# A chunked state-space scan rebuilt: blocks of eight chunks with 16 neighbouring columns, a doubling over the block ends, then the ends carried into the next block

## The chip, the cores and the metric

One core of one Trainium2 chip. The engines are TensorE (PE; its weight loads are listed as PEld), VectorE (DVE), ScalarE (ACT), GpSimd (POOL) and SyncE (SP), which issues most of the transfers. The metric is the device time of one execution in microseconds, the median of several runs.

## The reference, cut to what matters

One layer of a decoder: adaLN, a combined input projection, an S5 state-space branch beside a sliding-window attention branch, an output projection, then a gated MLP with a short convolution. x is (1, 1024, 1024) in float32. The change concerns the S5 branch alone. It has 32 groups of 16 channels, and each group drives 64 complex states through a linear recurrence over the 1024 positions:

```python
bu_re = jnp.einsum("blgh,gph->blgp", ug, bb_re)
bu_im = jnp.einsum("blgh,gph->blgp", ug, bb_im)
def combine(e1, e2):
    a1r, a1i, b1r, b1i = e1
    a2r, a2i, b2r, b2i = e2
    return (a2r * a1r - a2i * a1i,
            a2r * a1i + a2i * a1r,
            a2r * b1r - a2i * b1i + b2r,
            a2r * b1i + a2i * b1r + b2i)
_, _, s_re, s_im = lax.associative_scan(combine, (a_re_t, a_im_t, bu_re, bu_im), axis=1)
y = (jnp.einsum("blgp,ghp->blgh", s_re, c_re.astype(f32))
     - jnp.einsum("blgp,ghp->blgh", s_im, c_im.astype(f32))
     + d_skip.astype(f32).reshape(N_SSM_GROUPS, SSM_GROUP) * ug)
z = jax.nn.gelu(y.reshape(bsz, seq, D_SSM))
out = z * jax.nn.sigmoid(z @ w_glu.astype(f32) + b_glu.astype(f32))
```

## The kernel before

The 1024 positions are cut into 128 chunks of T = 8. Inside a chunk the recurrence is a small matrix (the local kernel); between chunks only the state at a chunk's end is carried. So the S5 branch has these stages. (1) The input U of each group is transposed, chunks along the free side, into UT (lines 534 to 548); ScalarE adds the shift Bu while it evacuates. (2) Products of WJ and UT give each chunk's contribution to the state, the injections, real in SR and imaginary in SI, for 16 pairs of groups and 128 chunks, with a column of zeros ahead (lines 562 to 579). (3) The scan over the 128 chunks, on VectorE (lines 645 to 681): a doubling up and down (six levels each), in which a step multiplies the columns at a power of two apart by a power of the transition and adds them to others. The helper cmac does it in pairs of instructions: a product into PSUM bank 7 (`bk<-tS,ep` in the rows), and its sum into the scan's tile (`tS<-tS,bk`). The powers stand in ep. (4) An exchange between the two halves of the partitions (lines 706 to 711). (5) For each group, y is the local kernel WI times UT plus the output matrix CA times the state, in PSUM, and its GELU on ScalarE gives zc (lines 714 to 726), which is transposed back into zT (lines 727 to 736). After it come the GLU (tanh on ScalarE, line 771), the split into high and low parts for the products, and the output projection.

Beside this run the attention heads: six projection tiles, three products each (high and low parts), then a norm per head on VectorE and ScalarE (head_w, head_out), and 16 attention units of four heads each (lines 811 to 861), whose exponentials are issued after the last GELU.

The local kernel needs a way over DRAM: ka, in tile A12, is written to kd by four transfers (line 623) and read back as WI (line 700). The relative-position bias takes the same way over vd (lines 603 to 605 and 629).

Tiles are named by tags; two uses of one tag share a buffer, and the later waits until the earlier is done. A scheduler decides the order of the instructions on each engine from the data they need. TensorE's order is pinned as written from line 524 to 581.

Of the kernel before, what the change touches and what calls it, by code (L numbers as in the profile page):

```python
# [20 lines left out]
NC_ = L // T  # L21
# [24 lines left out]
def pick(name, i):  # L46
    return PICK[name][i % len(PICK[name])]
# [15 lines left out]
def hymba_kernel(ctx, tc, xT, c, wmod, wu, wkvq, small, consts, relb, pq, wglu, wout, wup, wdn, out):  # L63
    nc = tc.nc
    pool = ctx.enter_context(tc.tile_pool(name="sb", bufs=1))
    pp = ctx.enter_context(tc.tile_pool(name="ps", bufs=1, space=bass.MemoryType.PSUM))
    dp = ctx.enter_context(tc.tile_pool(name="dr", bufs=1, space=bass.MemoryType.DRAM))
    bank = [pp.tile([128, 512], F32, name=f"bk{i}") for i in range(8)]
    SIZES = {"HA": 2048, "HB": 2048, "S16": 4128, "XQ": 4096}

    def new(tag, dt=F32):
        return pool.tile([128, SIZES.get(tag, 1024)], dt, tag=tag, name="t" + tag)

# [13 lines left out]
    vec, act, pol, sync = nc.vector, nc.scalar, nc.gpsimd, nc.sync  # L87
# [29 lines left out]
    def tt(eng, o, a, b, op):  # L117
        return eng.tensor_tensor(out=o, in0=a, in1=b, op=op)  # L118
# [106 lines left out]
    Bu = pool.tile([128, 32], F32, name="Bu")  # L225
# [13 lines left out]
    for k in range(8):  # L239
# [6 lines left out]
        w = half(newr(f"U{k}") if k < 4 else wux[:, (k - 4) * 1024:(k - 3) * 1024])  # L246
# [71 lines left out]
    PWr = pool.tile([128, 288], F32, name="PWr").rearrange("p (g d) -> p g d", d=9)  # L318
    PWi = pool.tile([128, 288], F32, name="PWi").rearrange("p (g d) -> p g d", d=9)
# [113 lines left out]
    for i in range(4):  # L433
        tmp = new("A10") if i == 3 else IB[i + 1]
# [102 lines left out]
    UTt = [None] * 4  # L537

    def emit_ut(i):
        if i % 2 == 0:  # L540
            UTt[i // 2] = new(f"A{5 + i // 2}")
        b = abank()
        for q in range(4):
            g = 4 * i + q
            pe.transpose(b[:, q * 128:(q + 1) * 128], U[:, g * 128:(g + 1) * 128], ident)
        for q in range(4):
            g = 4 * i + q
            act.activation(out=UTt[i // 2][:, (g % 8) * 128:(g % 8 + 1) * 128], in_=b[:, q * 128:(q + 1) * 128], func=AF.Identity, bias=Bu[:, g:g + 1])

    for i0, n_ in ((0, 4), (4, 2), (6, 2)):  # L550
        for i in range(i0, i0 + n_):
# [8 lines left out]
        return WJt[g // 8][:, (g % 8) * 128:(g % 8 + 1) * 128]  # L560

    scan = new("S16")
    SR = scan[:, 0:2064].rearrange("p (g c) -> p g c", c=129)
    SI = scan[:, 2064:4128].rearrange("p (g c) -> p g c", c=129)
    for i in range(4):
        br_, bi_ = abank(), abank()
        for q in range(4):
            for par in range(2):
                g = 2 * (4 * i + q) + par
                ps = slice(par * 64, par * 64 + 64)  # L570
                pe.matmul(br_[ps, q * 128:(q + 1) * 128], WJ(g)[:, 0:64], UT(g), start=True, stop=True)
                pe.matmul(bi_[ps, q * 128:(q + 1) * 128], WJ(g)[:, 64:128], UT(g), start=True, stop=True)
        next(h0)
        evac(SR[:, 4 * i:4 * i + 4, 1:129], br_.rearrange("p (g c) -> p g c", c=128), "I")
        if i != 1:
            next(h0)
        evac(SI[:, 4 * i:4 * i + 4, 1:129], bi_.rearrange("p (g c) -> p g c", c=128), "I")
    vec.memset(SR[:, :, 0:1], 0.0)
    vec.memset(SI[:, :, 0:1], 0.0)

    pst.close()

# [39 lines left out]
    for q in range(4):  # L622
        sync.dma_start(out=kd[:, 8 * q:8 * q + 8, 112:240],
                       in_=ka[32 * q:32 * q + 16, :].rearrange("p (g x) -> p g x", x=128))
# [17 lines left out]
        head_out(t, h, b)  # L642


    ep = pool.tile([128, 14 * 16], F32, name="ep")
    er = [ep[:, 16 * i:16 * i + 16] for i in range(6)]
    ei = [ep[:, 96 + 16 * i:112 + 16 * i] for i in range(6)]
    et = ep[:, 192:208]
    for par in range(2):
        ps = slice(par * 64, par * 64 + 64)  # L650
        vec.tensor_copy(out=er[0][ps, :], in_=PWr[ps, par:32:2, 8])
        vec.tensor_copy(out=ei[0][ps, :], in_=PWi[ps, par:32:2, 8])
    for l in range(1, 6):
        tt(vec, er[l], er[l - 1], er[l - 1], MUL)
        tt(vec, et, ei[l - 1], ei[l - 1], MUL)
        tt(vec, er[l], er[l], et, SUB)
        tt(vec, et, er[l - 1], ei[l - 1], MUL)
        tt(vec, ei[l], et, et, ADD)

    def cmac(l, dst, src, n):  # L660
        step = max(1, 512 // n)
        for g0 in range(0, 16, step):
            g1 = min(16, g0 + step)
            shp = [128, g1 - g0, n]
            tp = bank[7][:, 0:(g1 - g0) * n].rearrange("p (g c) -> p g c", c=n)
            e_r = er[l][:, g0:g1].rearrange("p (g o) -> p g o", o=1).to_broadcast(shp)
            e_i = ei[l][:, g0:g1].rearrange("p (g o) -> p g o", o=1).to_broadcast(shp)
            sr, si = SR[:, g0:g1, src], SI[:, g0:g1, src]
            dr, di = SR[:, g0:g1, dst], SI[:, g0:g1, dst]
            for d_, e_, s_, op in ((dr, e_r, sr, ADD), (dr, e_i, si, SUB), (di, e_r, si, ADD), (di, e_i, sr, ADD)):  # L670
                tt(vec, tp, s_, e_, MUL)
                tt(vec, d_, d_, tp, op)

    for l in range(6):
        s = 1 << l
        n = NC_ // (2 * s)
        cmac(l, slice(2 * s, 2 * s * n + 1, 2 * s), slice(s, 2 * s * (n - 1) + s + 1, 2 * s), n)
    for l in range(5, -1, -1):
        s = 1 << l
        n = NC_ // (2 * s) - 1  # L680
        cmac(l, slice(3 * s, 3 * s + 2 * s * (n - 1) + 1, 2 * s), slice(2 * s, 2 * s * n + 1, 2 * s), n)


    QS = {}
    for h in range(2):
        for i in range(4):
            q_ = newr(f"H{8 + 4 * h + i}")
            for kv in range(2):
                p0, p1 = slice(kv * 64, kv * 64 + 64), slice(64 - kv * 64, 128 - kv * 64)
                q = q_[:, kv * 512:kv * 512 + 512]  # L690
                QS[i, kv, h] = q
                src = qn[i][p0, h * 512:h * 512 + 512]
# [12 lines left out]

    for i in range(2):
        sw = new(f"U{4 + i}")[0:64, :].rearrange("p (g c) -> p g c", c=128)
        a_, b_ = SR[:, 8 * i:8 * i + 8, 1:129], SI[:, 8 * i:8 * i + 8, 1:129]
        act.copy(sw, a_[64:128])
        vec.tensor_copy(out=a_[64:128], in_=b_[0:64])  # L710
        act.copy(b_[0:64], sw)
# [4 lines left out]
    for i in range(8):  # L716
        b = bank[int(pick("YB", i))]
        for q in range(4):
            g = 4 * i + q
            o = b[:, q * 128:(q + 1) * 128]  # L720
            st = (SI if g % 2 else SR)[:, g // 2, 0:128]
            pe.matmul(o, UT(g), WI(g), start=True, stop=False)
            pe.matmul(o, st, CA(g)[:, 16:144], start=False, stop=True)
        zo = zc[i // 2].rearrange("p (t g h) -> p g t h", t=8, h=16)[:, 4 * (i % 2):4 * (i % 2) + 4]
        yb = b.rearrange("p (g t h) -> p g t h", t=8, h=16)
        gelus.append(act.activation(out=zo, in_=yb, func=AF.Gelu_apprx_tanh).ins)
    zTt = new("S16")
    zT = [zTt[:, m * 1024:(m + 1) * 1024] for m in range(4)]
    for m in range(4):
        zv = zT[m].rearrange("p (c t) -> p t c", t=8)  # L730
        for q2 in range(2):
            b = sbank()
            for q in range(4):
                t_ = 4 * q2 + q
                pe.transpose(b[:, q * 128:(q + 1) * 128], zc[m][:, t_ * 128:t_ * 128 + 128], ident)
            evac(zv[:, 4 * q2:4 * q2 + 4, :], b.rearrange("p (t c) -> p t c", t=4), "Z")

    cact2 = new("X4")
    sync.dma_start(out=cact2, in_=cad.partition_broadcast(128))
# [24 lines left out]
    for h in range(2):  # L764
        hs = slice(h * 512, h * 512 + 512)
        for n in range(4):
            b = sbank()
# [6 lines left out]
        for n in range(4):  # L774
            src = zT[n][:, hs]
# [31 lines left out]
    hp = ctx.enter_context(ExitStack())  # L807
    hp.enter_context(tc.high_priority(0))
    yT = [[new(f"U{2 * h + j}").rearrange("p (i t) -> p i t", i=2) for j in range(2)] for h in range(2)]
    att = pool.tile([128, 16 * 20], F32, name="att")  # L810
    for n in range(8):
        av = bank[2]
        for kv in range(2):
# [30 lines left out]
            for kb in range(nb):  # L844
                b = bank[3 + kb]
# [528 lines left out]
```

## Time and profile before

| | us |
|---|---|
| median of three runs | 1128.36 (1127.03 to 1128.59) |
| the profiled execution, its own time | 1126.86 |
| its span from the first to the last instruction | 1125.1 |
| TensorE busy in it | 1045.2 |
| VectorE busy | 923.1 |
| ScalarE busy | 581.7 |
| GpSimd busy | 275.7 |

The shares of the whole span mix stages with different limits. The stage of the scan lies between 95 and 275 us, and the rows below are from there. A timeline row gives the start in us, the time of the instruction or of a run of alike instructions (x and their number), the engine, the line, the operation with what it writes and reads, and in brackets how long the engine stood idle before it and what ended that.

### The profile page before, as it was taken

Reading aid. Unit: us, or ns where it says so; the run is one execution under the profiler, and the core shown is the slowest. Engines: PE = TensorE matmul, PEld = TensorE weight load, DVE = VectorE, ACT = ScalarE, POOL = GpSimd, SP = SyncE. Lnnn points to the kernel's source line nnn. Section 1 sums busy time; section 2 is a strip of 40 time slices with the busy share of each in tenths; the row PEclk is TensorE's granted clock in tenths of the full one; section 3 lists DMA queues with packets and bytes.
Section 4 is the critical chain, followed back from the end, with each engine's and each line's share of the span. In section 5 each row is a group of like instructions: output and inputs, shape, how many; then the busy total and the mean of one; then the engine's idle time right before and its main releaser. Section 6 shows DMA issues by size and latency. Waiting matters only on the chain.

```text
span 1125.1 us, 13333 instructions
## 1 busy us (share of the span) xinstructions
PE 1045.2 (93%) x4692; PEld 825.7 (73%) x4692; DVE 923.1 (82%) x1489; ACT 581.7 (52%) x1008; POOL 275.7 (25%) x165
## 2 busy tenths in 40 slices
PE   6979999589989799879999999999999999989998
PEld 4877777376656577657888888888888778768876
DVE  7994899958889587888777888887787888997985
ACT  5415443478896366636554545455545474434342
POOL 0000000001233102763222323221312033564541
PEclk9989999788999899979999999999999999999999
DMA  9501516014028855322223232332221449622012
GB/s 365 223 24 38 110 59 92 2 40 167 1 65 229 245 184 148 103 94 94 94 76 113 94 131 94 131 112 94 76 94 57 168 166 419 126 45 31 1 38 113
DMA packets 49638, 128.14 MB, mean 114 GB/s; under 512 B 6273, under 2 KB 14241, under 8 KB 49570
## 3 DMA queue, kind: packets, MB, share of 16 engines
q1 hardware_dynamic: 44962, 118.89, 31.0%
q0 software_dynamic: 4608, 8.39, 4.8%
q8 instruction: 37, 0.61, 0.2%
q14 instruction: 31, 0.25, 0.1%
HBM read 105.28 MB, written 21.99 MB: 113 GB/s over the span
## 4 chain that ended last, share of the span: by engine, by line
PE 46%; DVE 10%; issue 1%; DMA 1%; ACT 1%; POOL 0%; DVEq 0%; ACTq 0%; POOLq 0%
PE bk L97 45%; DVE tH L118 3%; DVE tA L118 2%; DVE tU L118 2%; DVE tX L127 1%; PE bk L99 1%; DMA tX<-in_dram 1%; DVE tX L118 1%; DVE tS L118 1%; DVE tXQ L127 0%; DVE tW L127 0%; DMA tW<-in_dram 0%; DVE tHA L118 0%; DVE tHB L118 0%; POOL tH L118 0%
## 5 line engine op out<-in xcount | busy, mean ns | idle before, releaser
L97 PE MATMUL bk<-tA,tU 128*128 128x512 f32 x516 | 127.2, 395 | 0.0
L97 PE MATMUL bk<-tU,tU 128*128 128x512 f32 x516 | 121.9, 390 | 1.6 <-DVE tU L118 1.1
L97 PE MATMUL bk<-tH,tU 128*128 128x512 f32 x477 | 116.0, 392 | 0.0
L97 PEld LDWEIGHTS bk<-tU,tU 128*128 128x128 f32 x516 | 96.5, 188 | 23.4 <-DVE tU L118 2.6
L97 PEld LDWEIGHTS bk<-tA,tU 128*128 128x128 f32 x516 | 97.0, 188 | 22.7
L97 PEld LDWEIGHTS bk<-tH,tU 128*128 128x128 f32 x477 | 89.1, 188 | 19.3
L127 DVE SCALAR_TENSOR_TENSOR tX<-tH,sm,tX 128x1023 f32<-128x1023 f32 x66 | 99.3, 1504 | 3.5 <-ACT tX L1100 3.4
L97 PE MATMUL bk<-tA,tXQ 128*128 128x512 f32 x300 | 74.5, 395 | 0.7 <-ACT tH L1053 0.7
L99 PE MATMUL bk<-tH,tU 128*128 128x512 f32 x267 | 65.7, 402 | 2.4 <-DVE tU L118 2.4
L133 ACT CAST tU<-tW 128x512 fp32r<-128x512 f32 (+1 forms) x67 | 47.1, 710 | 38.7 <-PE bk L97 18.2
L97 PEld LDWEIGHTS bk<-tA,tXQ 128*128 128x128 f32 x300 | 56.3, 188 | 14.2 <-ACT tH L1053 1.2
L118 POOL TENSOR_TENSOR tU<-tW,tU 128x512 fp32r<-128x512 f32 x25 | 36.1, 1455 | 114.9 <-ACT tU L133 93.2
L99 PEld LDWEIGHTS bk<-tH,tU 128*128 128x128 f32 x267 | 50.9, 193 | 15.4 <-DVE tU L118 3.2
L118 POOL TENSOR_TENSOR tXQ<-tW,tXQ 128x512 fp32r<-128x512 f32 x12 | 49.0, 4086 | 52.2 <-ACT tXQ L133 37.0
L118 DVE TENSOR_TENSOR tX<-tX,tX 128x512 f32<-128x512 f32 (+1 forms) x61 | 59.4, 976 | 1.0 <-DMA tX<-in_dram 0.2
L97 PE MATMUL bk<-tH,tA 128*128 128x512 f32 (+1 forms) x156 | 55.5, 487 | 5.0 <-ACT tH L133 2.1
L118 POOL TENSOR_TENSOR tH<-tH,att 128x1024 f32<-128x1024 f32 (+1 forms) x9 | 17.0, 1889 | 173.2 <-DVE att L841 153.3
L118 DVE TENSOR_TENSOR tU<-tW,tU 128x512 fp32r<-128x512 f32 (+2 forms) x43 | 37.7, 878 | 17.7 <-ACT tU L133 17.7
L97 PE MATMUL bk<-tXQ,tH 128*128 128x256 f32 (+2 forms) x224 | 50.2, 367 | 1.7 <-DVE att L829 1.6
L118 POOL TENSOR_TENSOR tU<-tX,tU 128x512 fp32r<-128x512 f32 x19 | 31.0, 1632 | 80.7 <-ACT tU L133 66.6
L97 PEld LDWEIGHTS bk<-tXQ,tH 128*128 128x128 f32 x224 | 44.4, 267 | 8.3 <-DVE att L829 4.4
L118 DVE TENSOR_TENSOR tU<-tX,tU 128x512 fp32r<-128x512 f32 x37 | 28.9, 788 | 23.6 <-ACT tU L133 23.6
(355 smaller groups left out, 2440.5 us busy)
## 6 DMA issues: line engine op xcount, KB each, us to landing
tW<-in_dram SPq DMA_DIRECT2D x49, 512.0 KB, 3.4
tX<-in_dram SPq DMA_DIRECT2D x47, 512.0 KB, 3.3
tS<-in_dram SPq DMA_DIRECT2D x30, 512.0 KB, 7.4
gd<-tX SPq DMA_DIRECT2D x22, 512.0 KB, 2.8
tA<-in_dram SPq DMA_DIRECT2D x12, 512.0 KB, 9.8
tH<-in_dram SPq DMA_DIRECT2D x12, 512.0 KB, 4.9
tH<-gd SPq DMA_DIRECT2D x8, 512.0 KB, 9.1
tA<-gd SPq DMA_DIRECT2D x8, 512.0 KB, 10.1
```

Of the source, the lines that this page charges most:

```text
L97: return f(*a, **k)
L99: i = f(*a, **k)
L118: return eng.tensor_tensor(out=o, in0=a, in1=b, op=op)
L127: return vec.scalar_tensor_tensor(out=o, in0=a, scalar=s, in1=b, op0=op0, op1=op1)
L133: act.copy(o, i)
```

## The change

The tile of the scan has another layout: real or imaginary (t), 16 pairs of groups (g), the chunk's place r in its block of eight, and the block q, 16 of them, with q innermost. So the 16 blocks are neighbouring columns. UT is written in that order, by r and then q; each injection's evacuation is cut into two copies (places 1 to 7 of all blocks, and place 0 of the next block), since the states are kept one chunk later; one memset on GpSimd clears the first column.

The scan has three parts. Six steps go from place r - 1 to place r for all 16 blocks, and a seventh carries the last place into the next block's place 0. Four steps double over the 16 block ends. Seven steps carry the ends into the other places. Each step is seven instructions: four products into mt, a tile in SBUF with the tag A12, one sum over both real and imaginary parts, and two over one part. The powers 1 to 8 of the transition over a chunk, and then 16, 32 and 64 of them, are made by epow. The exchange, the y products and the evacuation of zT read the new layout. The small tiles att and brow share a buffer.

```diff
-    SIZES = {"HA": 2048, "HB": 2048, "S16": 4128, "XQ": 4096}
+    SIZES = {"HA": 2048, "HB": 2048, "S16": 4096, "XQ": 4096}
...
-            act.activation(out=UTt[i // 2][:, (g % 8) * 128:(g % 8 + 1) * 128], in_=b[:, q * 128:(q + 1) * 128], func=AF.Identity, bias=Bu[:, g:g + 1])
+            act.activation(
+                out=UTt[i // 2][:, (g % 8) * 128:(g % 8 + 1) * 128].rearrange("p (r q) -> p q r", r=8), in_=b[:, q * 128:(q + 1) * 128].rearrange("p (q r) -> p q r", r=8),
+                func=AF.Identity, bias=Bu[:, g:g + 1],
+            )
...
+    SC = scan.rearrange("p (t g r q) -> p t g r q", t=2, g=16, r=8)
+    def evac_inj(t, i, b):
+        v = b.rearrange("p (g e q) -> p g e q", e=8, q=16)
+        evac(SC[:, t, 4 * i:4 * i + 4, 1:8, :], v[:, :, 0:7, :], "I")
+        evac(SC[:, t, 4 * i:4 * i + 4, 0, 1:16], v[:, :, 7, 0:15], "I")
...
-    vec.memset(SR[:, :, 0:1], 0.0)
-    vec.memset(SI[:, :, 0:1], 0.0)
+    pol.memset(SC[:, :, :, 0, 0:1], 0.0)
...
-    def cmac(l, dst, src, n):
-        step = max(1, 512 // n)
-        for g0 in range(0, 16, step):
-            g1 = min(16, g0 + step)
-            shp = [128, g1 - g0, n]
-            tp = bank[7][:, 0:(g1 - g0) * n].rearrange("p (g c) -> p g c", c=n)
...
-            for d_, e_, s_, op in ((dr, e_r, sr, ADD), (dr, e_i, si, SUB), (di, e_r, si, ADD), (di, e_i, sr, ADD)):
-                tt(vec, tp, s_, e_, MUL)
-                tt(vec, d_, d_, tp, op)
-    for l in range(6):
-        s = 1 << l
-        n = NC_ // (2 * s)
-        cmac(l, slice(2 * s, 2 * s * n + 1, 2 * s), slice(s, 2 * s * (n - 1) + s + 1, 2 * s), n)
-    for l in range(5, -1, -1):
...
+    def cmac(k, dst, src, n, tmp):
+        w = 16 * n
+        shp = [128, 16, n]
+        e_r, e_i = [v[:, k, :].rearrange("p (g o) -> p g o", o=1).to_broadcast(shp) for v in (epr, epi)]
+        ab_ = [[tmp[:, (2 * j + t) * w:(2 * j + t + 1) * w].rearrange("p (g q) -> p g q", q=n) for t in range(2)] for j in range(2)]
+        for t in range(2):
+            tt(vec, ab_[0][t], src[:, t], e_r, MUL)
+        tt(vec, ab_[1][0], src[:, 1], e_i, MUL)
+        tt(vec, ab_[1][1], src[:, 0], e_i, MUL)
+        both = tmp[:, 0:2 * w].rearrange("p (t g q) -> p t g q", t=2, q=n)
+        tt(vec, dst, dst, both, ADD)
+        tt(vec, dst[:, 0], dst[:, 0], ab_[1][0], SUB)
+        tt(vec, dst[:, 1], dst[:, 1], ab_[1][1], ADD)
+    mt = new("A12")
+    for r in range(2, 8):
+        cmac(0, SC[:, :, :, r, :], SC[:, :, :, r - 1, :], 16, mt)
+    cmac(0, SC[:, :, :, 0, 1:16], SC[:, :, :, 7, 0:15], 15, mt)
+    for l in range(4):
         s = 1 << l
+        cmac(7 + l, SC[:, :, :, 0, 1 + s:16], SC[:, :, :, 0, 1:16 - s], 15 - s, mt)
+    for r in range(1, 8):
+        cmac(r - 1, SC[:, :, :, r, 1:16], SC[:, :, :, 0, 1:16], 15, mt)
...
-        a_, b_ = SR[:, 8 * i:8 * i + 8, 1:129], SI[:, 8 * i:8 * i + 8, 1:129]
+        a_, b_ = [SC[:, t, 8 * i:8 * i + 8].rearrange("p g r q -> p g (r q)") for t in range(2)]
...
-            st = (SI if g % 2 else SR)[:, g // 2, 0:128]
+            st = SC[:, g % 2, g // 2].rearrange("p r q -> p (r q)")
...
-        zv = zT[m].rearrange("p (c t) -> p t c", t=8)
+        zv = zT[m].rearrange("p (q r t) -> p t r q", r=8, t=8)
```

The order of the instructions moves at three places that matter here. The first is VectorE's queue where the scan begins; tX are the heads' tiles, tA_892 and tA_899 are ka, tA_1493 is mt, tS_774 the scan's tile, bk_70 is bank 7. Before:

```order
L118 TENSOR_TENSOR tX_607<-bk_65,tX_362 128x512 [waits PE_49]
L118 TENSOR_TENSOR bk_70<-tS_774,ep 128x512 [waits DVE_49]
L118 TENSOR_TENSOR tS_774<-tS_774,bk_70 128x8x64 [waits DVE_49]
L118 TENSOR_TENSOR bk_70<-tS_774,ep 128x512 [waits DVE_49]
L118 TENSOR_TENSOR tS_774<-tS_774,bk_70 128x8x64 [waits DVE_49]
L118 TENSOR_TENSOR bk_70<-tS_774,ep 128x512 [waits DVE_49]
L118 TENSOR_TENSOR tA_892<-tA_892,ddt 128x8x16 [waits Activation_49]
L118 TENSOR_TENSOR tS_774<-tS_774,bk_70 128x16x32 [waits DVE_49]
```

Now:

```order
L118 TENSOR_TENSOR tX_607<-bk_65,tX_362 128x512 [waits PE_49]
L118 TENSOR_TENSOR tA_899<-tA_899,ddt 128x8x16 [waits Activation_49]
L127 SCALAR_TENSOR_TENSOR tX_601<-bk_68,tX_601 128x512 [waits PE_49,Activation_49]
L127 SCALAR_TENSOR_TENSOR tX_602<-tX_601,tX_602 128x512 [waits DVE_49]
L127 SCALAR_TENSOR_TENSOR tX_607<-tX_607,bcol,tX_602 128x512 [waits DVE_49]
L118 TENSOR_TENSOR tA_1493<-tS_774,ep 128x256 [waits DMAHW6_49,DMAHW7_49,DMAHW5_49,DMAHW4_49]
L118 TENSOR_TENSOR tA_1493<-tS_774,ep 128x256 x3
L122 TENSOR_SCALAR tX_607<-tX_607,kq 128x512 [waits DVE_49]
L118 TENSOR_TENSOR tX_607<-bk_66,tX_362 128x512 [waits PE_49]
L118 TENSOR_TENSOR tS_774<-tS_774,tA_1493 128x32x16 [waits DVE_49]
L118 TENSOR_TENSOR tU_1096<-tW_1093,tU_1095 128x1024 [waits Activation_49]
```

The first product of the scan stands behind the sum into ka, the first norm of the heads and four DMA queues, where before the scan's first level ran among them.

The second is TensorE's queue where the injections' operands are transposed; `cn` is the identity, tA_562 the second tile of IB, tS_382 is U, tHA and tHB are the first operands of the head product in bank 64. Before:

```order
L99 MATMUL bk_68<-cn,tA_561 128x128 x4
L97 MATMUL bk_64<-tHA,tU_1001 128x512 [waits Activation_49]
L97 MATMUL bk_64<-tHA,tU_1001 128x512
L99 MATMUL bk_69<-cn,tA_562 128x128 [waits DVE_49]
L99 MATMUL bk_69<-cn,tA_562 128x128 x3
L99 MATMUL bk_67<-cn,tA_562 128x128 x4
L99 MATMUL bk_68<-cn,tS_382 128x128 [waits Activation_49]
L99 MATMUL bk_68<-cn,tS_382 128x128 x3
```

Now (the rows end where the transposes begin again):

```order
L97 MATMUL bk_64<-tH_91,tU_1008 128x512
L97 MATMUL bk_64<-tH_92,tU_1008 128x512
L97 MATMUL bk_64<-tH_91,tU_1009 128x512
L97 MATMUL bk_64<-tH_93,tU_1008 128x512
L97 MATMUL bk_64<-tH_94,tU_1008 128x512
L97 MATMUL bk_64<-tH_93,tU_1009 128x512
L97 MATMUL bk_64<-tH_95,tU_1008 128x512
L99 MATMUL bk_69<-cn,tA_562 128x128 [waits DVE_49]
L99 MATMUL bk_69<-cn,tA_562 128x128 x3
L99 MATMUL bk_67<-cn,tA_562 128x128 x4
L99 MATMUL bk_68<-cn,tS_382 128x128 [waits Activation_49]
```

These twelve transposes stood after two of the head's products and stand after 19 of them now.

The third is ScalarE's queue at the end of the scan; L709 and L711 (before), L731 and L733 (now) are the exchange, L726 and L748 the GELU, L836 and L857 the attention's exponential. Before:

```order
L711 COPY tS_774<-tU_1649 64x8x128 [waits DVE_49,Activation_49]
L726 ACTIVATE tX_1655<-bk_69 128x4x8x16 [waits PE_49]
L726 ACTIVATE tX_1655<-bk_68 128x4x8x16 [waits PE_49]
L726 ACTIVATE tX_1656<-bk_69 128x4x8x16 [waits PE_49,Activation_49]
L836 ACT_TABLE_LOAD
L836 ACTIVATE att<-att 128x4 [waits DVE_49]
```

Now:

```order
L731 COPY tU_1678<-tS_774 64x1024 [waits DVE_49,Pool_49]
L731 COPY tU_1682<-tS_774 64x1024
L733 COPY tS_774<-tU_1678 64x1024 [waits DVE_49]
L733 COPY tS_774<-tU_1682 64x1024 [waits DVE_49]
L748 ACT_TABLE_LOAD
L748 ACTIVATE tX_1686<-bk_69 128x4x8x16 [waits PE_49]
L748 ACTIVATE tX_1686<-bk_70 128x4x8x16 [waits PE_49]
```

Both halves' exchanges stand together ahead of all eight GELUs, where the second half's stood behind four of them.

## Rows read from the trace of the kernel before

**Rows 1.** Table of stretches: limits, length, busy us (instructions) per engine, clock, DMA.

```profile
116.30:140.00 23.70, 23.70 (x221) 18.88 (x220) 22.36 (x32) 9.72 (x17) 0.00 (x0) 1.00 0.58 114
140.00:203.60 63.60, 57.81 (x292) 44.30 (x290) 61.45 (x128) 23.88 (x37) 0.00 (x0) 0.99 0.40 71
203.60:230.20 26.60, 19.11 (x69) 13.64 (x70) 25.45 (x48) 17.00 (x26) 0.00 (x0) 0.63 0.00 1
...
248.00:273.00 25.00, 22.71 (x98) 16.59 (x99) 18.16 (x52) 24.69 (x62) 1.89 (x1) 0.75 0.44 148
350.00:400.00 50.00, 43.23 (x169) 30.51 (x168) 35.10 (x58) 21.49 (x34) 11.41 (x12) 0.93 0.85 241
```

**Rows 2.** Timeline of VectorE, scan and heads, 116 to 230 us.

```profile
116.36 0.70 DVE L118 TENSOR_TENSOR bk<-tS,ep 128x512 f32<-128x512 f32 x1 [6.80 <-ACT tS L133]
...
137.64 0.68 DVE L118 TENSOR_TENSOR tX<-bk,tX 128x512 f32<-128x512 f32 x1
...
138.63 1.22 DVE L118 TENSOR_TENSOR tU<-tW,tU 128x1024 fp32r<-128x1024 f32 x1
...
139.97 1.05 DVE L118 TENSOR_TENSOR bk<-tS,ep 128x512 f32<-128x512 f32 x1
...
229.51 0.68 DVE L118 TENSOR_TENSOR tS<-tS,bk 128x504 f32<-128x504 f32 x1
```

**Rows 3.** VectorE: scan groups by width (busy us, mean ns), then two timeline rows.

```profile
L118 DVE TENSOR_TENSOR bk<-tS,ep 128x512 f32<-128x512 f32 x12 | 10.0, 832 | 7.7 <-ACT tS L133 7.3
L118 DVE TENSOR_TENSOR tS<-tS,bk 128x512 f32<-128x512 f32 x12 | 9.9, 821 | 0.3
...
L118 DVE TENSOR_TENSOR tS<-tS,bk 128x16 f32<-128x16 f32 x4 | 0.7, 186 | 0.1
...
92.94 0.45 DVE L118 TENSOR_TENSOR tA<-tU,PWr 128x288 f32<-128x288 f32 x1
55.12 9.10 DVE L118 TENSOR_TENSOR tA<-tU,PWi 128x1024 f32<-128x1024 f32 x8
```

**Rows 4.** SyncE's timeline from the bias table to kd; a transfer's us to landing.

```profile
128.60 0.36 SPq L605 DMA_DIRECT2D vd<-tA  x1
...
134.51 0.36 SPq L629 DMA_DIRECT2D tA<-vd  x1
135.00 1.85 SPq L623 DMA_DIRECT2D kd<-tA  x4
...
kd<-tA SPq DMA_DIRECT2D x4, 64.0 KB, 3.7
```

**Rows 5.** Timeline of ScalarE: activations into UT, a plain and a strided copy.

```profile
101.95 3.20 ACT L548 ACTIVATE tA<-bk,Bu 128x128 f32<-128x128 f32 x12 [3.31 <-PE bk L99]
...
154.37 0.57 ACT L133 COPY tA<-bk 128x512 f32<-128x512 f32 x1
...
247.90 1.10 ACT L133 COPY tS<-bk 128x512 f32<-128x512 f32 x1
```

**Rows 6.** Timeline of ScalarE, TensorE and GpSimd from the exchange on.

```profile
204.34 1.04 ACT L709 COPY tU<-tS 64x1024 f32<-64x1024 f32 x1 [0.59 <-DVE tH L118]
...
225.28 0.63 PE L97 MATMUL bk<-tHA,tA 128*128 128x128 f32 x2
...
231.28 0.39 PE L97 MATMUL bk<-tA,tS 128*128 128x128 f32 x2
...
240.92 1.28 ACT L836 ACT_TABLE_LOAD   x1
...
245.49 0.60 ACT L133 CAST tHB<-tW 128x512 fp32r<-128x512 f32 x1
...
247.41 0.60 ACT L726 ACTIVATE tX<-bk 128x512 f32<-128x512 f32 x1
...
244.54 1.04 POOL L118 TENSOR_TENSOR tH<-tH,att 128x512 f32<-128x512 f32 x1 [131.87 <-DVE att L841]
...
355.56 2.77 POOL L118 TENSOR_TENSOR tH<-tH,att 128x1024 f32<-128x1024 f32 x1
```

More of the change, by code (lines that the diff above doesn't have):

```diff
@@ L456, in hymba_kernel @@
     bcol = pool.tile([128, 6], F32, name="bcol")
-    brow = pool.tile([2, 128 * 2], F32, name="brow")
+    att = pool.tile([128, 16 * 20], F32, name="att")
+    brow = att[0:2, 64:320]
     def head_w(t):
@@ L562, in hymba_kernel @@
     scan = new("S16")
-    SR = scan[:, 0:2064].rearrange("p (g c) -> p g c", c=129)
-    SI = scan[:, 2064:4128].rearrange("p (g c) -> p g c", c=129)
+    SC = scan.rearrange("p (t g r q) -> p t g r q", t=2, g=16, r=8)
[3 more added lines that the diff above has]
+        evac(SC[:, t, 4 * i:4 * i + 4, 0, 1:16], v[:, :, 7, 0:15], "I")
     for i in range(4):
@@ L573, in hymba_kernel @@
         next(h0)
-        evac(SR[:, 4 * i:4 * i + 4, 1:129], br_.rearrange("p (g c) -> p g c", c=128), "I")
+        evac_inj(0, i, br_)
         if i != 1:
             next(h0)
-        evac(SI[:, 4 * i:4 * i + 4, 1:129], bi_.rearrange("p (g c) -> p g c", c=128), "I")
-    vec.memset(SR[:, :, 0:1], 0.0)
-    vec.memset(SI[:, :, 0:1], 0.0)
+        evac_inj(1, i, bi_)
+    pol.memset(SC[:, :, :, 0, 0:1], 0.0)
     pst.close()
@@ L642, in hymba_kernel @@
         head_out(t, h, b)
[L645 to L648, printed above, removed]
+    ep = pool.tile([128, 416], F32, name="ep")
+    epr = ep[:, 0:176].rearrange("p (n g) -> p n g", g=16)
+    epi = ep[:, 176:352].rearrange("p (n g) -> p n g", g=16)
     for par in range(2):
         ps = slice(par * 64, par * 64 + 64)
-        vec.tensor_copy(out=er[0][ps, :], in_=PWr[ps, par:32:2, 8])
-        vec.tensor_copy(out=ei[0][ps, :], in_=PWi[ps, par:32:2, 8])
@@ L653, in hymba_kernel @@
[L653 to L658, printed above, removed]
-    def cmac(l, dst, src, n):
-        step = max(1, 512 // n)
-        for g0 in range(0, 16, step):
-            g1 = min(16, g0 + step)
-            shp = [128, g1 - g0, n]
-            tp = bank[7][:, 0:(g1 - g0) * n].rearrange("p (g c) -> p g c", c=n)
[L666 to L669, printed above, removed]
-            for d_, e_, s_, op in ((dr, e_r, sr, ADD), (dr, e_i, si, SUB), (di, e_r, si, ADD), (di, e_i, sr, ADD)):
-                tt(vec, tp, s_, e_, MUL)
-                tt(vec, d_, d_, tp, op)
@@ L674, in hymba_kernel @@
-    for l in range(6):
-        s = 1 << l
-        n = NC_ // (2 * s)
-        cmac(l, slice(2 * s, 2 * s * n + 1, 2 * s), slice(s, 2 * s * (n - 1) + s + 1, 2 * s), n)
-    for l in range(5, -1, -1):
-        s = 1 << l
-        n = NC_ // (2 * s) - 1
-        cmac(l, slice(3 * s, 3 * s + 2 * s * (n - 1) + 1, 2 * s), slice(2 * s, 2 * s * n + 1, 2 * s), n)
+        vec.tensor_copy(out=epr[ps, 0, :], in_=PWr[ps, par:32:2, 8])
+        vec.tensor_copy(out=epi[ps, 0, :], in_=PWi[ps, par:32:2, 8])
@@ new lines, in epow @@
+    def epow(dst, n, src, by):
+        o = ep[:, 352:352 + 16 * n].rearrange("p (n g) -> p n g", g=16)
+        xr, xi = epr[:, src:src + n], epi[:, src:src + n]
+        yr, yi = [v[:, by:by + 1].to_broadcast([128, n, 16]) for v in (epr, epi)]
+        dr, di = epr[:, dst:dst + n], epi[:, dst:dst + n]
+        tt(vec, dr, xr, yr, MUL)
+        tt(vec, o, xi, yi, MUL)
+        tt(vec, dr, dr, o, SUB)
+        tt(vec, di, xr, yi, MUL)
+        tt(vec, o, xi, yr, MUL)
+        tt(vec, di, di, o, ADD)
@@ new lines, in hymba_kernel @@
+    for args in ((1, 1, 0, 0), (2, 2, 0, 1), (4, 4, 0, 3), (8, 1, 7, 7), (9, 1, 8, 8), (10, 1, 9, 9)):
+        epow(*args)
+    def cmac(k, dst, src, n, tmp):
[11 more added lines that the diff above has]
+        tt(vec, dst[:, 1], dst[:, 1], ab_[1][1], ADD)
@@ L735, in hymba_kernel @@
                 pe.transpose(b[:, q * 128:(q + 1) * 128], zc[m][:, t_ * 128:t_ * 128 + 128], ident)
-            evac(zv[:, 4 * q2:4 * q2 + 4, :], b.rearrange("p (t c) -> p t c", t=4), "Z")
+            evac(zv[:, 4 * q2:4 * q2 + 4], b.rearrange("p (t r q) -> p t r q", t=4, r=8), "Z")
     cact2 = new("X4")
@@ L809, in hymba_kernel @@
     yT = [[new(f"U{2 * h + j}").rearrange("p (i t) -> p i t", i=2) for j in range(2)] for h in range(2)]
-    att = pool.tile([128, 16 * 20], F32, name="att")
     for n in range(8):
```

## The prediction

> **What bounds the kernel now.** I read the table of stretches first [rows 1]. [...] From 248 to 273 us ScalarE is the bound: 24.69 of 25.00. The chain of waits, followed back from the end, stops long before it reaches this place, so the scan has to be followed by hand, from the rows of each engine in order of time. The scan's first instruction starts at 116.36 and its last at 229.51, ending at 230.2 [rows 2].
>
> **The change part by part.**
>
> *The scan's own work.* Before: 112 VectorE instructions in 22 groups of one width, of which the first and the last are shown [rows 3]; their busy times add up to 62.6 us. A pair with columns at distance 2 costs 0.70 us for 512 elements (one at 116.36) [rows 2], at distance 4 it costs 1.05 (one at 139.97) [rows 2]. After: 18 steps of 7 instructions, 126 in all: in six steps four products of 256 elements, one sum over 512 and two over 256; in eight steps 240 and 480; in four steps 224, 208, 176, 112 and their doubles. All of them run over neighbouring columns. Prices: 0.45 us for 288 elements [rows 3], 0.70 for 512, which is about 1.1 ns an element and 0.13 fixed; so 0.42 for 256, 0.41 for 240, 0.66 for 480. A full step is 6 x 0.42 + 0.70 = 3.2 us, one of 240 is 3.1, the four narrow ones together 10.4. Sum: 6 x 3.2 + 8 x 3.1 + 10.4 = 54.6 us. That is the upper bound. The lower: eight instructions of 1024 elements that wait for nothing take 9.10 us, 1.14 each, where one alone is listed with 1.22 [rows 3], so about 0.08 of an instruction lies under the next; for up to 110 of the 126 that makes 46. So the scan saves 8 to 16.5 us of VectorE; I take 14, since about half of the new instructions carry no wait and the heads' work stands between the others. [...]
>
> *The powers of the transition* (36 small instructions in place of 25) lie in VectorE's idle time ahead of 116 us, where only the scan's input is awaited (idle 6.80) [rows 2]. Cost 0; without that cover 11 more at 0.19, the price of 16 elements [rows 3], some 2 us.
>
> *A new wait.* The products went into PSUM bank 7, which nobody else used then. Now they go into tile A12, which holds the local kernel matrix (ka) until four writes have carried it to kd. The order shows the first product waiting for four DMA queues. Those writes are issued at 135.00 to 136.85, behind the first bias load at 134.51, which itself waits for the bias table's write issued at 128.60; the last of them lands 3.7 us after its issue at about 136.4 [rows 4]. So the scan can't start before T0 = 140.1, where before it started at 116.36. Behind the waiting product in VectorE's queue stand three head instructions that before ran from 137.64 to 139.85, 2.2 us [rows 2], among them the low half of the next head's weights, for which TensorE waits. What VectorE did by 140 and now does after it: 24 scan instructions of 512 elements (10.0 + 9.9 us [rows 3]) less the two that came after (2.1), that is 17.8, and the 2.2 of heads.
>
> *What feeds the scan* comes later by 0 to 6 us. (a) The 32 activations that write the transposed input now write at a distance of 64 bytes. No row shows that; the nearest is the copy that writes at 32 bytes: 1.10 us for 512 elements against 0.57 for the plain copy [rows 5]. By it a block of 128 loses 0.13 us, and 28 of the 32 stand in a stretch where ScalarE goes from one to the next (twelve in 3.20 us [rows 5]): 0 to 3.6. [...] (b) In TensorE's order the transposes behind the first eight now stand after some 17 head products. Before, ScalarE idled 3.31 us while those ran and had two copies and four activations done already [rows 5]; now these 2.2 us come after: 0 to 2. (c) Each evacuation is split in two (448 and 60 elements): 0 to 0.4. I take 4.5 of the 6, so T0 = 144.6.
>
> *The scan's end.* Before, 230.2 - 140.0 = 90.2 us of VectorE from T0 on. After: 90.2 + 17.8 + 2.2 - 14 = 96.2. End at 144.6 + 96.2 = 240.8, that is 10.6 later (4 to 15).
>
> *The halves no longer overlap.* Before, the scan's last level ran in two halves of the groups, and the exchange of the first half began at 204.34 [rows 6], so half of the y products and GELUs were done when the scan ended. [...] I put the last GELU's end 12.5 us after the scan's end (11.5 to 13.5), at 253.3. Before it ended at 248.0, but by then two attention units' exponentials had been done, from the table load at 240.92 to 245.49 [rows 6], 3.3 us without the load, and 0.6 less of a cast remained now. Compared at the same state: 253.3 + 3.3 - 0.6 = 256.0 against 248.0, 8 us later.
>
> *Behind that* ScalarE is 99% busy, so nothing is made up at once, and the modulation loads that fill the DMA queues from 350 to 400 us (share 0.85 [rows 1]) wait for the buffer that this path frees. The memset that moved to GpSimd costs nothing; that engine is idle until 244.54 us [rows 6].
>
> **Sum.** 8 us on the profiled execution's own 1126.86 us gives 1134.9. The median of the three runs shown is 1128.36, the profiled one 1.5 below it; I put the forecast at 1135.5.
>
> **The rivals.**
>
> *Faster: the GLU gets ahead.* In ScalarE's order before, six attention units' exponentials stand ahead of the first GLU tanh, now about four and a half; and two of 14 table loads (1.28 us [rows 6]) are gone. GpSimd's multiplication of the first unit starts at 244.54, that of the last at 355.56 [rows 6], so a unit took 111 / 15 = 7.4 us. If what frees the buffer for the modulation loads is the GLU alone, this gives back up to 1.5 x 7.4 + 2.6 = 13.7 us against the 8 lost: 1128.4 - 5.7, say 1123. It decides from 10.3 us given back on, where the time falls 0.2% under the one before. For it: the DMA share of 0.85 at 350 to 400. Against it: TensorE and VectorE are busy there too and the attention units still have to be done before the output projection. Chance 0.2.
>
> *No change.* The feeding terms are 0, the saving is at its end of 16.5 and the last GELU comes 11.5 behind: 8 - 4.5 - 2.5 - 1 = 0. 1128.4. Also if half of the GLU's gain comes. Chance 0.15.
>
> *Much slower: TensorE starves behind the wait.* The weights' low half stands behind the first products and the first sum, so TensorE has no head product from about 141 to T0 + 3 = 147.6. It then has most of the 57.8 us left that it was busy with from 140.0 to 203.6 [rows 1], and VectorE 96, of which the heads' part waits for TensorE. If the two no longer interleave, VectorE idles 5 to 10 us more: 1140 to 1146, say 1143. Against it: VectorE has the scan to do meanwhile. Chance 0.15.
>
> *It doesn't do what it says:* neighbouring columns may be no cheaper than the strided ones. The 512-element pairs at 0.70 against 1.05 speak against that; it lies in the range as the upper bound of 54.6.
>
> **How the numbers follow.** Forecast 0.5, its own range 1130.5 to 1142. The range takes in the no-change case and most of the other two: 1125.5 to 1144.5. About 0.2% (2.3 us) is what a measurement of this kernel can tell from no change. Faster is the first rival, 0.2; same is the second, 0.15, and a little of the forecast's lower edge, 0.02; slower is the rest, 0.63.
>
> **What would show each step.** The first product into tA from tS, at 140 or later, with VectorE idle ahead of it, and its releaser a DMA; before 130 the new wait is wrong. The 256-element products at 0.42 and their spacing at 0.33 to 0.46. The activations into the transposed input at 0.29 (no penalty) or 0.42. The scan's end near 241 and the last GELU near 253. If the first copy of zT comes at 253 and the modulation loads still start by 341, the first rival is right. The prediction is wrong if the scan ends before 232, or if the first output projection comes no later than before.

## The result, and the profile after

The changed kernel takes 1145.71 us (1145.26 to 1147.21, 4 runs), beside 1128.46 for the kernel before (4 runs): a ratio of 1.0158, 95% interval 1.0138 to 1.0177. That is 17.3 us slower where 7 were forecast, 1.2 us above the upper end of the range. The profiled execution took 1145.26 us, its span is 1143.5.

The table of stretches of the changed kernel, with the limits of [rows 1]:

```profile
116.30:140.00 23.70, 23.70 (x243) 18.74 (x243) 3.12 (x5) 9.90 (x24) 0.24 (x2) 1.00 0.49 81
140.00:203.60 63.60, 61.91 (x311) 47.91 (x310) 59.58 (x142) 25.55 (x38) 0.00 (x0) 1.00 0.50 85
203.60:230.20 26.60, 12.57 (x26) 6.74 (x26) 26.16 (x61) 11.55 (x18) 0.00 (x0) 0.53 0.05 5
230.20:248.00 17.80, 11.81 (x75) 11.44 (x76) 10.84 (x36) 8.33 (x10) 0.00 (x0) 0.65 0.00 0
248.00:273.00 25.00, 18.07 (x114) 15.17 (x113) 9.66 (x26) 20.69 (x50) 2.08 (x2) 0.73 0.42 135
```

The reader is to see two holes. From 116.3 to 140 VectorE is busy 3.12 us where it was busy 22.36 [rows 1]. And from 248 to 273 ScalarE is busy 20.69 us where it was busy 24.69: it now waits there for the y products.

VectorE's timeline of the changed kernel: the first products of the scan, its last sums, and the first of the two copies of the exchange.

```profile
143.28 1.44 DVE L118 TENSOR_TENSOR tA<-tS,ep 128x256 f32<-128x256 f32 x4 [4.92 <-DMA kd<-tA]
...
236.27 0.72 DVE L118 TENSOR_TENSOR tS<-tS,tA 128x240 f32<-128x240 f32 x2
...
238.52 0.69 DVE L732 COPY tS<-tS 64x1024 f32<-64x1024 f32 x1
```

The new wait stands in the first row's bracket: what ended VectorE's idle time is the write to kd. SyncE's timeline shows why it comes at 143.28: the bias table's write (L615) is issued at 132.44, 3.84 us later than before, since the injections are evacuated later; the first bias load behind it waits until 138.03, and the four writes to kd stand behind that one [rows 4]. Of the 3.84 us, 1.66 stand already at the first of the transposes (93.09 in the execution of before, 94.75 in this one). They are not the change's: over the traces of all twelve kernels, with the old scan or the new, that point lies anywhere between 93.1 and 95.2. So marks of single executions are good to some 2 us.

```profile
132.44 0.36 SPq L615 DMA_DIRECT2D vd<-tA  x1
138.03 0.36 SPq L639 DMA_DIRECT2D tA<-vd  x1
138.51 1.85 SPq L633 DMA_DIRECT2D kd<-tA  x4
```

The scan's groups on VectorE (busy us, mean ns), the three largest of 17:

```profile
L118 DVE TENSOR_TENSOR tA<-tS,ep 128x240 f32<-128x240 f32 x32 | 11.8, 400 | 0.2
L118 DVE TENSOR_TENSOR tA<-tS,ep 128x256 f32<-128x256 f32 x24 | 8.8, 418 | 5.0 <-DMA kd<-tA 4.9
L118 DVE TENSOR_TENSOR tS<-tS,tA 128x240 f32<-128x240 f32 x16 | 5.8, 400 | 0.1
```

All 17 sum to 49.2 us, against 62.6 before [rows 3]: 13.4 less.

Behind the scan, ScalarE's timeline has the table load for the GELUs, the first and the last GELU, and TensorE's the first y products, those where its clock has risen, and the last:

```profile
241.29 1.28 ACT L748 ACT_TABLE_LOAD   x1
243.85 0.60 ACT L748 ACTIVATE tX<-bk 128x512 f32<-128x512 f32 x1 [1.28 <-PE bk L97]
...
256.76 0.59 ACT L748 ACTIVATE tX<-bk 128x512 f32<-128x512 f32 x1
...
239.87 0.63 PE L97 MATMUL bk<-tA,tS 128*128 128x128 f32 x2
...
242.76 0.39 PE L97 MATMUL bk<-tHA,tA 128*128 128x128 f32 x2
...
255.51 0.39 PE L97 MATMUL bk<-tA,tS 128*128 128x128 f32 x2
```

The scan ends at 237.0, 6.8 us later than before, and the last GELU at 257.35, 20.3 us behind it. TensorE had been busy 12.57 of the 26.60 us from 203.6 to 230.2, at a granted clock of 0.53 of full speed, near the 0.50 that it shows from 206 to 242.6 us. Each row of two instructions is one product. The first six took 0.63 us, at a granted clock of 0.50, and stand 0.43 us apart; from 242.76 on they take 0.39, at 1.00, and stand 0.22 apart. So the lower clock costs some 1.3 us of the tail.

### The profile page after: what moved, and what is told of

Same layout as the page of the kernel before. It is cut to its first block, busy times and chain, and to the rows that moved or that the text cites. A ratio compares the mean times of both kernels' runs of the same rounds, so it can differ in the third digit from the quotient of the medians.

```text
span 1143.5 us, 13346 instructions
## 1 busy us (share of the span) xinstructions
PE 1053.0 (92%) x4692; PEld 826.2 (72%) x4692; DVE 913.5 (80%) x1512; ACT 580.9 (51%) x1014; POOL 273.3 (24%) x166
## 4 chain that ended last, share of the span: by engine, by line
PE 44%; DVE 11%; DMA 1%; issue 1%; POOL 1%; ACT 1%; POOLq 0%; SPq 0%; DVEq 0%; ACTq 0%
PE bk L97 44%; DVE tH L118 3%; DVE tA L118 2%; DVE tU L118 2%; DMA tX<-in_dram 1%; DVE tX L127 1%; DVE tX L118 1%; DVE tS L118 1%; POOL tU L118 1%; DVE tXQ L127 0%; DVE tW L127 0%; DMA tW<-in_dram 0%; ACT tU L133 0%; DVE tXQ L118 0%; DVE tHA L118 0%
## 5 line engine op out<-in xcount | busy, mean ns | idle before, releaser
L97 PE MATMUL bk<-tXQ,tH 128*128 128x256 f32 (+2 forms) x224 | 53.0, 384 | 14.2 <-DVE att L850 9.8
L97 PEld LDWEIGHTS bk<-tXQ,tH 128*128 128x128 f32 x224 | 45.8, 274 | 23.0 <-DVE att L850 12.7
## 6 DMA issues: line engine op xcount, KB each, us to landing
tA<-in_dram SPq DMA_DIRECT2D x12, 512.0 KB, 10.2
```

What stands on the lines that cost most here:

```text
L97: return f(*a, **k)
```

## The experiments

Three kinds of runs: one takes the wait away or puts it into the old scan, one joins or splits the ends of the two halves, one leaves the scan out. In the summary at the end of this section their marks stand side by side.

**The wait taken away.** The local kernel matrix ka goes to A9, which is free at about 128 us; mt stays in A12, which then has no pending transfer.

```diff
-    ka = new("A12")
+    ka = new("A9")
```

> The changed kernel with the local kernel matrix in buffer A9 (free at about 128 us) in place of A12, so that the scan's products need not wait for the four writes to kd. Theory A (the time goes with the end of the scan and of the last GELU, one for one): in the changed kernel VectorE idles about 12.8 of the 15.8 us between the last injection copy (127.2) and the first product (143.28); these come back. First product near 127.5, scan end near 224 (237.0 in the changed kernel), last GELU near 244.5 (257.4), time 1145.7 - 12.8 = 1133. Rival C (the heads' products on TensorE would hold VectorE anyway): scan end 232 or later, time 1140 or more. Rival B (what is lost lies behind the GELUs, in the order of attention and GLU): scan end near 224, but the time hardly moves, 1143 to 1146.

Measured: 1125.19 us, ratio to the kernel before 0.9966 (0.9949 to 0.9983). One buffer's name turns 17.3 us lost into 3 to 4 us gained: the move is worth some 20 us, more than the whole loss. VectorE's timeline of this kernel:

```profile
126.97 1.43 DVE L118 TENSOR_TENSOR tA<-tS,ep 128x256 f32<-128x256 f32 x4 [25.83 <-ACT tS L133]
...
211.29 0.71 DVE L118 TENSOR_TENSOR tS<-tS,tA 128x240 f32<-128x240 f32 x2
```

The start is where it was expected (126.97), and its releaser is now the last injection's copy on ScalarE. The scan's end, 212.0, comes 25 us earlier than with the wait, though the start is only 16.3 earlier. The 12.8 us that were expected were too few. What differs in the rows: with the wait only 3 us of attention's work stand behind the scan in VectorE's queue, without it 16 us of heads' and attention work do, and they cover the exchange and the first y products.

**The control.** The kernel before with the same move of ka, where nothing waited for it.

> Control: the kernel before with only the local kernel matrix moved to buffer A9, where nothing waited for it. If the move of that buffer brings nothing by itself, as theory A needs: 1127 to 1130. Rival: it frees something else (the bias tables' loads then wait for the writes to kd), and a part of the 20.5 us between the changed kernel and the one with A9 is not the scan's wait: under 1124 or over 1132.

Measured: 1126.67 us, ratio 0.9976 (0.9958 to 0.9995). So the move alone brings 2.7 us, 0.6 to 4.7: a little more than the "nothing" that was expected. Of the 20 us at least 15 are the scan's wait.

**The wait alone, in the old scan.** The old scan's products go into A12 instead of bank 7.

```diff
-            tp = bank[7][:, 0:(g1 - g0) * n].rearrange("p (g c) -> p g c", c=n)
+            tp = mt[:, 0:(g1 - g0) * n].rearrange("p (g c) -> p g c", c=n)
```

> The kernel before, with its old scan, its products put into A12 in place of PSUM bank 7: the wait alone, in the old scan. With the other three (before: neither; the changed scan with the matrix in A9: the new scan without the wait, 1125.2; the changed kernel: both, 1145.7) it makes a table of two by two. Theory A (the wait costs about 20 us whatever the scan): first product near 140, 1146 to 1149. Rival (the new scan, which runs from one end to the other and overlaps nothing, is what makes the wait dear): 1128.4 plus 4 to 10.

Measured: 1153.67 us, ratio 1.0217 (1.018 to 1.0254), 24.5 us. The wait is dear in either scan; the rival falls. That the products now go to SBUF in place of PSUM costs nothing itself: the scan's groups sum to 61.4 us against 62.6. VectorE's timeline:

```profile
140.11 0.69 DVE L118 TENSOR_TENSOR tA<-tS,ep 128x512 f32<-128x512 f32 x1 [4.79 <-DMA kd<-tA]
...
251.52 0.68 DVE L118 TENSOR_TENSOR tS<-tS,tA 128x504 f32<-128x504 f32 x1
```

The old scan needs 112.1 us from its first product to its end under the wait, the new one 93.7 (143.28 to 237.0). In time the new scan brings 6.7 us with the wait (1.0217 to 1.0158). Without it, it is 3.8 us (1 to 0.9966), of which the control's 2.7 come from the move of ka alone; the 1.1 us left are not clear of noise. So 13.4 us of VectorE's time saved bring the whole kernel little.

**The halves' ends joined, in the kernel before.** The two loops of a level are swapped, so that both halves of the last level end together. The same instructions, in another order.

```diff
-        for g0 in range(0, 16, step):
-            ...
-            for d_, e_, s_, op in ((dr, e_r, sr, ADD), (dr, e_i, si, SUB), (di, e_r, si, ADD), (di, e_i, sr, ADD)):
-                tt(vec, tp, s_, e_, MUL)
-                tt(vec, d_, d_, tp, op)
+        for which in range(4):
+            for g0 in range(0, 16, step):
+                ...
+                tt(vec, tp, s_, e_, MUL)
+                tt(vec, d_, d_, tp, op)
```

> The kernel before with the two half loops of a scan level swapped (the four products outermost, the halves of the groups inside), so that both halves of the last level end together and the exchange, the y products and the GELUs all come behind the scan's end; the same instructions, nothing else. Theory A (the un-overlapped tail costs what the changed kernel shows, 20 us from the scan's end to the last GELU): scan end 230, last GELU 250.5 with no attention unit done ahead of it, which stands 5 us behind the kernel before at the same state: about 1133.5. Rival: the tail is hidden by other work, 1127.5 to 1129.

Measured: 1143.33 us, ratio 1.0118 (1.0086 to 1.0149). Joining the ends costs 13.3 us where 5 were expected. VectorE's last sum and ScalarE's last GELU:

```profile
237.64 0.67 DVE L118 TENSOR_TENSOR tS<-tS,bk 128x504 f32<-128x504 f32 x1
...
254.95 0.59 ACT L727 ACTIVATE tX<-bk 128x512 f32<-128x512 f32 x1
```

The scan's end came 8.1 us later as well, since attention's and heads' work that stood behind it now stands between its instructions; the GELUs follow 17.2 us behind it. So the 13.3 us are not the tail alone: both the later end and the longer tail are in them.

**The halves split, in the changed kernel.** The last seven steps for groups 0 to 7, then for 8 to 15, first as 49 more instructions, with the wait and without:

```diff
-    for r in range(1, 8):
-        cmac(r - 1, SC[:, :, :, r, 1:16], SC[:, :, :, 0, 1:16], 15, mt)
+    for gs in (slice(0, 8), slice(8, 16)):
+        for r in range(1, 8):
+            cmac(r - 1, SC[:, :, gs, r, 1:16], SC[:, :, gs, 0, 1:16], 15, mt, gs)
```

> The changed kernel with its last seven steps run for groups 0 to 7 first and then for groups 8 to 15, so that the first half's exchange and products lie under the second half; the wait on the writes stays. 49 more instructions cost VectorE 2.5 to 6 us. Theory A (tail behind the scan not overlapped): scan end near 241 (237.0), last GELU 12 us behind it instead of 20.3, near 253 (257.4), time 1145.7 - 4.4 = about 1141. Rival B (the loss lies behind the GELUs): 1145 to 1146.

> Both edits: local kernel matrix in A9, last seven steps in two halves. Theory A, terms add: scan end near 228, last GELU near 240, time about 1129. Rival C (TensorE's heads hold the scan): 1136 or more. Rival B: 1142 or more.

Measured: 1144.12 us (1.0155, 1.012 to 1.0189) with the wait, 1137.25 (1.0078, 1.0055 to 1.01) without. Both are misses. With the wait the scan ends 7.1 us later than in the changed kernel (244.1), not 4, and that eats the overlap. Without it the scan ends at 233.7, where the unsplit one ended at 212.0: the second half's small instructions stand among the heads' and attention's on VectorE, to the end. It lies 12 us above the unsplit version. At the first GLU tanh it is 9.7 us behind that one (279.7 against 270.0), at the load into the buffer that zT frees 20.3 (357.1 against 336.8); why the order there came out worse was not followed.

So the same split was made cheaply: all seven steps in one, eight instructions of 840 elements for each half, 16 in place of 49. The core of it:

```diff
+        for dt_, st_, et_, op in ((0, 0, 0, ADD), (0, 1, 1, SUB), (1, 1, 0, ADD), (1, 0, 1, ADD)):
+            tt(vec, tp, s_[st_], e_[et_], MUL)
+            tt(vec, d_[dt_], d_[dt_], tp, op)
```

Here tp, s_, e_ and d_ have the shape 8 groups by 7 places by 15 blocks; the source is repeated over the places and the power over the blocks.

> The changed kernel, its wait on the writes kept, with the last seven steps as eight instructions of 840 elements for each half of the groups (16 in place of 49), so that the first half's exchange and products can lie under the second half. Theory A (the un-overlapped tail is about half of what the change costs): scan end near 232 (237.0), the last GELU 13 us behind it (20.3), near 245, time 245 + 887 = 1132. Rival (in the changed kernel the tail is long for another reason, the clock or the order of ScalarE's queue): scan end near 232, last GELU near 252, 1139.

> Local kernel matrix in A9, and the last seven steps as eight instructions of 840 elements for each half of the groups (16 in place of 49). At about 1.1 ns an element and 0.13 fixed they take 16.8 us where the seven steps take 21.7. Theory A: scan end near 219, last GELU near 231 to 233, time 1120 to 1122. Rival C (TensorE becomes the bound before the scan's end): 1126 to 1130. Rival B: 1140 or more.

With the wait kept: 1133.18 us, ratio 1.0048 (1.0034 to 1.0063), 12.4 us under the changed kernel. The rows are clearer than was hoped: the scan's end did not move at all.

```profile
236.00 1.03 DVE L118 TENSOR_TENSOR tS<-tS,tA 128x840 f32<-128x840 f32 x1
...
244.75 0.60 ACT L755 ACTIVATE tX<-bk 128x512 f32<-128x512 f32 x1 [1.73 <-PE bk L97]
245.36 1.28 ACT L864 ACT_TABLE_LOAD   x1
...
251.85 0.60 ACT L755 ACTIVATE tX<-bk 128x512 f32<-128x512 f32 x1
```

It ends at 237.0 as in the changed kernel; what changed is the tail: the seventh GELU ends at 245.35, 8.3 us behind the scan. So in the changed kernel, too, the lost overlap costs up to 12 us. It is an upper bound, since the edit does a second thing: its scan groups sum to 45.5 us where the changed kernel's sum to 49.2, and the room went to heads' and attention work ahead of the scan's end.

Without the wait: 1123.54 us, ratio 0.995 (0.9933 to 0.9968), the fastest of those that compute the scan, but not clear of the version with ka in A9 alone. The scan ends at 208.5, 3.5 us earlier, and the last GELU at 239.1, no earlier.

**The floor.** The version with ka in A9, its 126 scan instructions left out.

> The changed kernel with the local kernel matrix in A9 and the scan's 126 instructions left out (the chunks' states are then not carried over, only the powers of the transition are still formed). It gives the floor that the heads and attention set without the scan. Theory A with VectorE the bound to the end of the heads: the heads' end and the last GELU come 35 to 45 us earlier than with the scan, time under 1100. Rival C (from some point TensorE's heads are the bound, as the version with merged halves hints, whose GELUs ended no earlier): last GELU 225 or later, time 1108 to 1120.

Measured: 1119.01 us, ratio 0.9905 (0.9872 to 0.9939); the last GELU ends at 232.4. Rival C holds: without the wait the new scan stands some 6 us above the time without any scan, so the merged halves could bring little there. From 140 to 203 us it is TensorE with the heads' products that sets this floor: it is busy 62.81 of 63.00 us, VectorE 31.63:

```profile
140.00:203.00 63.00, 62.81 (x320) 48.58 (x317) 31.63 (x54) 26.86 (x41) 0.00 (x0) 1.00 0.47 88
```

**How to compare at the last GELU.** The kernel before, with all eight GELUs ahead of attention's first exponentials, as the changed kernel has them.

```diff
-            with tc.issue_after(gelus[7]):
+            with ExitStack() as st_:
+                for g_ in gelus:
+                    st_.enter_context(tc.issue_after(g_))
```

> The kernel before with all eight GELUs set ahead of the attention's first exponentials in ScalarE's order, as the changed kernel has them (before, two attention units and two table loads stand between the seventh and the eighth). It tests how the kernels must be compared at the last GELU. Where all GELUs come first, time minus the last GELU's end was 886.3 to 888 us in five kernels (886.4 in the one without the scan, 887.3 with the matrix in A9, 884.6 with the merged halves, 885.5 before with one end, 888.0 in the changed kernel, 886.1 before with the wait). Theory D (the prediction compared wrongly: two units ahead are worth about 8 us, not 2.7): last GELU near 242.6 and time 242.6 + 886.5 = 1129, no change or up to 2 us slower, though the last GELU ends 5.4 us earlier. The prediction's own comparison (2.7 us for two units ahead): 2.7 us gained, 1125.5.

Measured: 1128.64 us, ratio 0.9996 (0.9981 to 1.0012). The last GELU ends at 244.9 where it ended at 248.0, and the time is the same; the gain of 2.7 us that the prediction's comparison asks for lies outside the interval. (The profiled execution took 1132.31 us, 3.7 above the median, and was 2.0 us late at the scan's first product already.) Its scan's last sum on VectorE and its last GELU on ScalarE:

```profile
231.52 0.68 DVE L118 TENSOR_TENSOR tS<-tS,bk 128x504 f32<-128x504 f32 x1
...
244.32 0.59 ACT L726 ACTIVATE tX<-bk 128x512 f32<-128x512 f32 x1
```

So with halves that overlap, and the GELUs in the changed kernel's order, the tail is 12.7 us (232.2 to 244.9), where the changed kernel's is 20.3.

**The marks side by side** (us; time is that of the profiled execution; in all seven kernels the eight GELUs come ahead of attention's exponentials):

| | first product | scan's end | last GELU's end | time | time less GELU |
|---|---|---|---|---|---|
| scan left out, ka in A9 | - | - | 232.4 | 1118.85 | 886.4 |
| ka in A9 | 126.97 | 212.0 | 238.85 | 1126.15 | 887.3 |
| ka in A9, merged halves | 125.84 | 208.5 | 239.1 | 1123.74 | 884.6 |
| before, GELUs first | 118.40 | 232.2 | 244.9 | 1132.31 | 887.4 |
| before, one end | 117.26 | 238.3 | 255.5 | 1140.94 | 885.4 |
| changed kernel | 143.28 | 237.0 | 257.35 | 1145.26 | 887.9 |
| before, with the wait | 140.11 | 252.2 | 266.1 | 1152.20 | 886.1 |

Over 34 us of the last GELU the time follows it one for one, within 1.7 us. In these seven nothing is made up behind it and little is added. It doesn't hold for every order: with the 49 more instructions and ka in A9 the time less the seventh GELU's end (243.2) is 895.4, where it is 886.0 before.

## Why the prediction was wrong

The direction, the wait, and the saving were right; one term, the tail behind the scan, was mis-sized, and its sign in the sum was wrong.

*The scan's own work* was right: 13.4 us saved, 14 taken. The 256-element products stand at 0.34 us from one to the next (four in 1.44, the last with its full 0.42), listed with 0.42. The listed times of all 126 sum to 53.7 us, and VectorE is busy with them for 49.2: part of an instruction's time lies under its neighbour, as in the row of eight [rows 3].

*The wait* was right: first product at 143.28 (144.6 forecast), released by the write to kd. The way there was another than I wrote. The activations into UT lost almost nothing, 9.3 us for the 32 against 8.9. So writes at a distance of 64 bytes cost almost nothing here, while the copies into zT, now at 256 bytes, take 1.07 us where they took 1.13 at 32. What makes those twice as slow as a plain copy (0.57 [rows 5]) stays open. The 4.5 us that I gave the feeding terms came out as 3.84 at the bias table's write, and with it the kd writes. Of these 1.66 are no term of mine, as said above. Another 2.0 arise until TensorE takes up the twelve transposes of U that stand behind the head products (101.32 before, 104.96 now): my term (b), at its upper end; in four of the six other executions with this order it is 3.6. That leaves 0.2 for (a) and (c).

*The scan's end* was forecast 10.6 us later and came 6.8 later: 1.3 from the earlier first product, and 93.7 us from there to the end where I had 96.2. This error was to the good and hid a part of the next one.

*The halves no longer overlap* is the step that failed, twice. First its size: the 12.5 us of the sum were my estimate, most of it 60 products at 0.63 or 0.39 us a pair [rows 6], 9 to 11 us. No run shows that term. A row of two instructions is one product and not a pair of products. The 64 products are 128 instructions (two are missing in the trace of the changed kernel), of which all but four come behind the scan. So 62 products follow, the first six 0.43 us apart and the others 0.22, which is 15 us and not 9 to 11:

```profile
L97 PE MATMUL bk<-tA,tS 128*128 128x128 f32 x64 | 12.9, 290 | 0.0
L97 PE MATMUL bk<-tHA,tA 128*128 128x128 f32 x30 | 7.4, 334 | 6.4 <-DVE tX L127 6.4
L97 PE MATMUL bk<-tHB,tA 128*128 128x128 f32 x32 | 6.2, 275 | 0.0
```

With transposes and attention's products between them TensorE works from 239.87 to 255.90, 16.0 us, and the tail is 20.3. Second the comparison: I set the last GELU of before, 248.0 [rows 6], equal to 245.3, because two attention units stood ahead of it. But that GELU only stood behind them in ScalarE's queue; seven were done at 240.9:

```profile
240.30 0.60 ACT L726 ACTIVATE tX<-bk 128x512 f32<-128x512 f32 x1 [1.72 <-PE bk L97]
```

By the table above (time less 886.5) the kernel before, 1126.86, has its mark at 240.4. So its tail was 10.2 us, not 15.1. Directly, without the time in it, the run with the GELUs first has 12.7.

The sum as it should have been: scan's end +6.8, tail 20.3 - 10.2 = +10.1, together 16.9, measured 17.3. That this comes out proves little, because the 10.2 was taken from the time; the direct 12.7 makes the tail +7.6 and the sum 14.4. The run with the GELUs first is the like-for-like comparison: scan's end +4.8, tail +7.6, together 12.4, and the two profiled executions lie 13.0 us apart (1132.31, 1145.26). The sum as it was: +10.6, tail 12.5 - 15.1 = -2.6, together 8. I had an overlap removed and the tail shorter for it; had I written the tail of before and after side by side, the sign would have shown it. The two experiments on the tail, 12.4 and 13.3 us, each move something else too, so they show its sign and its order of size: it is 8 to 10 us, where I had -2.6.

*Behind that* nothing is made up, as forecast. The load into the buffer that zT frees, the first of the modulation loads, is issued at 340.76 in the trace of before, at 356.46 in the changed one, and at 336.75 with ka in A9:

```profile
356.46 0.34 SPq L915 DMA_DIRECT2D tS<-cad  x1
```

But this load is no mark for the time. With the GELUs first it is issued at 333.05, 7.7 us earlier than before, and the kernel is no faster; with ka in A9 and merged halves at 326.49, 10.3 us ahead of ka in A9 alone, and that is worth 2.4 us of the two executions. So the part of my reasoning that let the time go by these loads isn't borne out.

*The rivals.* The GLU did not get ahead: that load came 15.7 us later, not by 341. TensorE did not starve VectorE: VectorE is busy 59.58 of the 63.60 us from 140 on, of which the wait until 143.28 is most of the rest. That this rival's time, 1143, lies near the measured one is chance. "No change" fell with the tail.

## What to carry to other kernels

When a chain that ended in halves is rebuilt to end at once, write down the tail from its last instruction to the next bound before and after; the tail gets longer by what ran beneath the second half, here 8 to 10 us, most of the 13.4 that the arithmetic saved. A temporary that moves from a private buffer into a shared tag inherits every pending transfer of that tag: here one name cost some 15 to 20 us, and another free buffer gave it back. To compare two kernels at a mark, take a mark that no queue order delays (here the seventh GELU is better than the eighth), and test on several kernels that the time follows it.

## What the runs showed of the hardware

Activations of 128 elements that write at a distance of 64 bytes take nearly the time of plain ones (32 of them 9.3 us for 8.9), though a copy of 512 elements that writes at 32 bytes takes 1.10 us beside 0.57 for a plain one [rows 5]. VectorE's products over 8 x 7 x 15 elements, with a source repeated over one dimension and a factor over another, take 1.03 us for 840 elements, and so do the sums, which have no repeated operand. Beside the 0.68 us of the changed kernel's sums over 512 elements that is 1.07 ns for each further one, so neither repetition costs anything that shows.
